# Layer 2's feed-forward up projections as seven quarter products instead of eight

## The chip, the cores and the metric

The kernel runs on one core of a Trainium2 chip. The core has five engines that work from queues of their own, each in order: TensorE (PE) for matmuls, VectorE (DVE), ScalarE (ACT), GpSimd (POOL) and SyncE (SP), which issues most DMA transfers here. The metric is the device time of one execution in microseconds (us); lower is better.

## The reference, cut to what matters

Two layers of a diffusion backbone over 512 latent tokens of width 1024, with 256 context tokens. Each layer has token mixers, an output projection with a gated residual, and a SwiGLU feed-forward part with 2816 inner columns. The change is in the second layer, where only the 512 latent tokens are still needed:

```python
def _swiglu(h, w1, w3, w2):
    return (jax.nn.silu(h @ w1) * (h @ w3)) @ w2
...
x = x + ga1 * (o @ w_out)
h2 = _rmsnorm(x, g_norm2) * (1.0 + sc2) + sh2
x = x + ga2 * _swiglu(h2, w_ff1, w_ff3, w_ff2)
```

All of it is in float32.

## The kernel before, in words

Activations lie transposed: 128 partitions hold 128 of the 1024 features, eight such tiles (k = 0 to 7) make the width, and tokens lie along the free dimension. A float32 product is made from three matmuls in a faster format (fp32r). Each operand is split into a high part (a cast) and a low part (the operand minus its high part), and `mm3` (the matmul is its line L241) issues high x high, high x low and low x high into one PSUM tile. Activations are split once; weights are split when they come in. `weights` does that: a transfer from SP's queue into a `raw` tile of 128 x 1024 (two buffers), a cast on ACT to `hi` (L231) and a subtraction on POOL to `lo` (L232), each with four buffers. It is shared by all weights of the program.

`dense` does the output projection and the feed-forward part of a layer. For layer 2 it first finishes the output projection in two halves of 256 tokens, with the sums of squares for the norm on the way; `norm_apply` then makes the scaled rows `xn` (DVE, L329) and the high (ACT, L331) and low part (DVE, L332) of h2 in two big tiles. The feed-forward loop goes over 22 blocks f of 128 inner columns, in groups of 3 or 4 (FF_CUTS). For each f, 8 k x 3 matmuls of 512 columns make the block of h2 @ w1 and as many that of h2 @ w3, each in a PSUM tile of its own. ACT applies Silu (L1331), DVE multiplies (L1332), ACT and DVE split the result into `gh` (L1335) and `gl` (L1337). After the group, `down` adds up its blocks' products with w2 for each of the eight output tiles, and `update` (DVE, L1248) multiplies by the gate and adds to x, in place. The last group's updates are followed by the transfers to the output.

What is issued when is decided by a scheduler at build time, which fixes an order for each engine; on the chip each engine runs its own queue in that order and waits on semaphores. A pool's buffer is given again when all that use its former tile are done. Only weights are marked as of high priority.

## Time and profile before

| what | value |
|---|---|
| median of 3 runs | 1828.52 us (1824.92 to 1829.95) |
| profiled execution, its own time | 1835.55 us |
| its span, first to last instruction | 1833.8 us |
| mean granted TensorE clock in it | 0.967 |
| PE, DVE, ACT, POOL busy in the span | 94%, 53%, 29%, 30% |

The profile comes from one execution, which took 7.0 us longer than the median of the runs; 1.75 us of its time lie outside the span. Busy times of an engine are sums over its instructions, and matmuls overlap each other, so the pace of matmuls is read from their starts and not from their durations. The granted clock is TensorE's, as a share of 2.4 GHz; it has two levels, 2.4 and 1.2 GHz.

### The profile page before, as it was taken

Reading aid. Unit: us, or ns where it says so; the run is one execution under the profiler, and the core shown is the slowest. Engines: PE = TensorE matmul, PEld = TensorE weight load, DVE = VectorE, ACT = ScalarE, POOL = GpSimd, SP = SyncE. Lnnn points to the kernel's source line nnn. Section 1 sums busy time; section 2 is a strip of 40 time slices with the busy share of each in tenths; the row PEclk is TensorE's granted clock in tenths of the full one; section 3 lists DMA queues with packets and bytes.
Section 4 is the critical chain, followed back from the end, with each engine's and each line's share of the span. In section 5 each row is a group of like instructions: output and inputs, shape, how many; then the busy total and the mean of one; then the engine's idle time right before and its main releaser. Section 6 shows DMA issues by size and latency. Waiting matters only on the chain.

```text
span 1833.8 us, 25688 instructions
## 1 busy us (share of the span) xinstructions
PE 1725.8 (94%) x10142; PEld 1395.3 (76%) x10142; DVE 969.5 (53%) x2259; ACT 527.2 (29%) x852; POOL 558.6 (30%) x360
## 2 busy tenths in 40 slices
PE   5899999898999999999899998989999999999999
PEld 2667877566878888888678877778767787787887
DVE  7988535572177445446956346265666632232332
ACT  2422234452241211121121223323444432222221
POOL 4553200201221322231643512423111244344442
PEclk7999989999999999999899998989999999999999
DMA  8355340414135434343342332332322123233222
GB/s 337 103 155 165 128 167 24 167 53 182 38 125 151 127 127 153 107 154 110 106 110 75 106 112 81 132 110 89 114 64 64 47 92 93 77 107 103 93 92 81
DMA packets 83065, 207.25 MB, mean 113 GB/s; under 512 B 15360, under 2 KB 35968, under 8 KB 82816
## 3 DMA queue, kind: packets, MB, share of 16 engines
q1 hardware_dynamic: 54160, 160.44, 26.9%
q0 software_dynamic: 7824, 29.38, 4.8%
q10 hardware_dynamic: 20960, 15.78, 2.8%
q8 instruction: 80, 1.31, 0.3%
q14 instruction: 41, 0.34, 0.1%
HBM read 185.68 MB, written 21.99 MB: 113 GB/s over the span
## 4 chain that ended last, share of the span: by engine, by line
PE 76%; DVE 15%; issue 4%; ACT 2%; POOL 1%; DMA 1%; ACTq 0%; DVEq 0%; POOLq 0%
PE psD L241 54%; PE psD L703 4%; PE psS L932 3%; PE psT L241 2%; PE psQ L979 1%; PE psQ L990 1%; PE psT L376 1%; PE psS L801 1%; POOL lo L232 1%; PE psT L856 1%; PE psQ L1045 1%; DVE ro L662 1%; PE psQ L1030 1%; PE psT L278 1%; PE psT L1067 1%
## 5 line engine op out<-in xcount | busy, mean ns | idle before, releaser
L232 POOL TENSOR_TENSOR lo<-raw,hi 128x1024 fp32r<-128x1024 f32 (+1 forms) x178 | 432.2, 2434 | 875.5 <-ACT hi L231 875.2
L241 PE MATMUL psD<-big,hi 128*128 128x512 f32 (+1 forms) x2368 | 605.9, 360 | 12.2 <-ACT big L331 5.7
L241 PEld LDWEIGHTS psD<-big,hi 128*128 128x128 f32 x2368 | 399.8, 191 | 88.1 <-ACT big L331 8.1
L231 ACT CAST hi<-raw 128x1024 fp32r<-128x1024 f32 (+1 forms) x178 | 184.2, 1039 | 774.5 <-PE psD L241 466.6
L241 PE MATMUL psD<-big,lo 128*128 128x512 f32 (+1 forms) x1184 | 368.2, 359 | 1.2 <-POOL lo L232 1.2
L241 PEld LDWEIGHTS psD<-big,lo 128*128 128x128 f32 x1184 | 202.9, 191 | 38.4 <-POOL lo L232 2.7
L1332 DVE TENSOR_TENSOR sg<-sg,psD 128x768 f32<-128x768 f32 (+1 forms) x44 | 36.1, 820 | 308.8 <-PE psD L241 300.5
L241 PE MATMUL psD<-gh,hi 128*128 128x512 f32 (+1 forms) x528 | 163.6, 359 | 4.9 <-DVE xb L1248 4.7
L241 PE MATMUL psD<-gl,hi 128*128 128x512 f32 (+1 forms) x528 | 165.8, 360 | 0.0
L241 PE MATMUL psD<-gh,lo 128*128 128x512 f32 (+1 forms) x528 | 163.6, 358 | 0.0
L1248 DVE SCALAR_TENSOR_TENSOR xb<-psD,mod,xb 128x512 f32<-128x512 f32 (+1 forms) x112 | 64.7, 613 | 114.9 <-PE psD L241 114.8
L1337 DVE TENSOR_TENSOR gl<-sg,gh 128x768 fp32r<-128x768 f32 (+1 forms) x44 | 99.2, 2254 | 39.5 <-ACT gh L1335 39.5
L407 DVE CUSTOM_DVE_ANT_0 junk<-wmt,cb,pcol 128x1024 f32<-128x1024 f32 x64 | 97.1, 1517 | 27.3 <-DMA wmt<-in_wmodT 26.2
L241 PEld LDWEIGHTS psD<-gh,hi 128*128 128x128 f32 x528 | 89.5, 189 | 24.4 <-DVE xb L1248 8.5
L241 PEld LDWEIGHTS psD<-gh,lo 128*128 128x128 f32 x528 | 90.1, 189 | 16.6 <-issue 0.2
L241 PEld LDWEIGHTS psD<-gl,hi 128*128 128x128 f32 x528 | 89.8, 189 | 15.8 <-issue 0.4
L1248 DVE SCALAR_TENSOR_TENSOR xq<-psD,mod,xq 128x512 f32<-128x512 f32 (+1 forms) x64 | 42.2, 682 | 78.6 <-PE psD L241 78.6
L932 PE MATMUL psS<-k,q 64*128 64x256 f32 (+1 forms) x432 | 78.2, 336 | 3.4 <-DVE mx L1019 3.0
L241 PE MATMUL psD<-h,hi 128*128 128x512 f32 (+1 forms) x288 | 76.2, 350 | 4.2 <-ACT h L331 2.7
L932 PEld LDWEIGHTS psS<-k,q 64*128 64x128 f32 x432 | 58.1, 195 | 23.6 <-issue 9.1
L241 PEld LDWEIGHTS psD<-h,hi 128*128 128x128 f32 x288 | 50.7, 194 | 15.4 <-ACT h L331 3.2
L241 PE MATMUL psD<-on,hi 128*128 128x256 f32 (+1 forms) x176 | 51.6, 331 | 1.3 <-ACT on L1081 1.3
(396 smaller groups left out, 2494.5 us busy)
## 6 DMA issues: line engine op xcount, KB each, us to landing
raw<-in_w_ff SPq DMA_DIRECT2D x132, 512.0 KB, 3.5
wmt<-in_wmodT SPq DMA_DIRECT2D x48, 512.0 KB, 3.6
wm<-in_wmod SPq DMA_DIRECT2D x28, 512.0 KB, 6.0
raw<-in_winT SPq DMA_DIRECT2D x18, 512.0 KB, 3.6
room<-in_wmod SPq DMA_DIRECT2D x12, 512.0 KB, 11.4
nab<-in_nab SPq DMA_DIRECT2D x8, 640.0 KB, 4.2
rot<-trot POOLq DMA_DIRECT2D x8, 576.0 KB, 6.0
cf<-in_four POOLq DMA_DIRECT2D x8, 520.0 KB, 4.9
```

The lines of the kernel that those rows point to most:

```text
L231: nc.scalar.copy(hi, raw)
L232: nc.gpsimd.tensor_sub(lo, raw, hi)
L241: nc.tensor.matmul(o, lhsT=lhs[i], rhs=rhs[j][..., s], start=start and n == 0, stop=stop and n == 2)
L278: self.nc.tensor.matmul(dst, lhsT=src, rhs=self.ident, start=True, stop=True)
L376: nc.tensor.matmul(ps[32 * j:32 * j + 32], lhsT=self.cvec[:, k], rhs=ws[k // 2][:, k % 2], start=half == 0, stop=half == 1)
L407: nc.vector.tensor_tensor_reduce(junk, w, cb[:, i], 1.0, self.pcol[1][:, PC_B + f:PC_B + f + 1], op0=ALU.mult, op1=ALU.add, accum_out=mod[ ...
L662: v.tensor_mul(er[:, :, :, o], er[:, :, :, s], bcr)
L703: nc.tensor.matmul(ps, lhsT=h[i][:, k, tk], rhs=w[j][:, k % per], start=k == 0 and q == 0, stop=k == KT - 1 and q == 2)
L932: self.nc.tensor.matmul(dst, lhsT=q2[i][h, qc], rhs=view(k2[j][h]), start=n == 0, stop=n == 2)
L1248: self.nc.vector.scalar_tensor_tensor(x[:, m, sl], ps[:, sl], gate[:, m, i:i + 1], x[:, m, sl], op0=ALU.mult, op1=ALU.add)
L1332: nc.vector.tensor_mul(sg, sg, pp[1])
L1337: marks.append(nc.vector.tensor_sub(gl, sg, gh))
```

## The change

Layer 2 gets a function of its own, `dense_last`, in place of `dense`. Two inner blocks, f and f + 11, are made together. Seen as 2 x 2 quarters, the weights of such a pair are a11, a12 (block f, features 0 to 511 and 512 to 1023) and a21, a22 (block f + 11); the activations are b11, b21, b12, b22 (features by halves, tokens by halves of 256). Seven products of quarter size replace eight, in Winograd's form of Strassen's scheme: four sums of weight quarters (s1 to s4, on DVE, in each round), four sums of activation quarters (t1 to t4, made once before the loop, in place in the tile of x), and seven additions behind the products. A quarter product is 4 k x 3 matmuls of 256 columns.

Weights of w1 and w3 are loaded by `load_halves` into `raw` and a second tile `raw2` (two buffers, in the loop's own pool), and split by `split_weight`, which makes the low part on DVE (L1371) where `weights` has it on POOL. w2 still goes through `weights`. The residual after the output projection is written to a tile of its own (`xr`) instead of over x. The down projection takes the two blocks of a pair at once and adds to `xr`; it uses the two PSUM tiles that were the norm's, and the up products have six instead of four.

```diff
@@ -1363,6 +1363,176 @@
+    def split_weight(self, src, n):
+        nc = self.nc
+        hi = self.whi.tile([P, n], F32R, name="hi")
+        lo = self.wlo.tile([P, n], F32R, name="lo")
+        nc.scalar.copy(hi, src)
+        nc.vector.tensor_sub(lo, src, hi)
+        return [(hi[:, i:i + 512], lo[:, i:i + 512]) for i in range(0, n, 512)]
+
+    def load_halves(self, fp, src, f):
+        nc = self.nc
+        with self.tc.high_priority():
+            ra = self.raw.tile([P, 1024], F32, name="raw")
+            rb = fp.tile([P, 1024], F32, name="raw2", bufs=2)
+            for t, g in ((ra, f), (rb, f + NFF // 2)):
+                nc.sync.dma_start(t, src[g].rearrange("p k c -> p (k c)"))
+        return ra, rb
+
+    def split_halves(self, fp, raws, part):
+        v = self.nc.vector
+        a1, a2 = (raws[0][:, i:i + 512] for i in (0, 512))
+        b1, b2 = (raws[1][:, i:i + 512] for i in (0, 512))
+        with self.tc.high_priority():
+            if part == 0:
+                return self.split_weight(raws[0], 1024)
+            if part == 3:
+                return self.split_weight(b2, 512)
+            s = fp.tile([P, 1024], F32, name="ssum", bufs=4)
+            if part == 1:
+                v.tensor_add(s[:, :512], b1, b2)
+                v.tensor_sub(s[:, 512:], s[:, :512], a1)
+                self.s2 = s[:, 512:]
+            else:
+                v.tensor_sub(s[:, :512], a1, b1)
+                v.tensor_sub(s[:, 512:], a2, self.s2_of)
+            return self.split_weight(s, 1024)
+
+    def dense_last(self, l, cl, on, x, hp, x_dst, parts):
...
+        res = hp.tile([P, KT, SEQ], F32, name="xr")
...
+                v.scalar_tensor_tensor(res[:, m, sl], ps[:, sl], mod[:, 16 + m, 0:1], x[:, m, sl],
+                                       op0=ALU.mult, op1=ALU.add)
...
+        def operand(name, src, gp):
+            hi, lo = (hp.tile([P, 4, HN], F32R, name=f"{name}{i}") for i in "hl")
+            nc.scalar.copy(hi, src)
+            (nc.gpsimd if gp else v).tensor_sub(lo, src, hi)
+            return hi, lo
+
+        B = {}
+        gsc = self.gsc[l][1]
+        for j, (pb, (sl, _)) in enumerate(zip(pbs, parts)):
+            for i in range(2):
+                for k in range(4 * i, 4 * i + 4):
+                    xn = self.xn.tile([P, NT], F32, name="xn")[:, :HN]
+                    v.scalar_tensor_tensor(xn, res[:, k, sl], gsc[:, k, 0:1], pb[:, :HN], op0=ALU.mult, op1=ALU.mult)
+                    nc.scalar.activation(x[:, k, sl], xn, AF.Identity, bias=sh[:, k, 0:1])
+                B[i, j] = x[:, 4 * i:4 * i + 4, sl]
+        ops = {1: operand("b11", B[0, 0], False), 2: operand("b21", B[1, 0], True)}
+        t1, t2, t3, t4 = B[0, 0], B[1, 1], B[0, 1], B[1, 0]
+        v.tensor_sub(t1, B[0, 1], B[0, 0])
+        ops[5] = operand("t1", t1, False)
+        v.tensor_sub(t3, B[1, 1], B[0, 1])
+        ops[3] = operand("b22", B[1, 1], True)
+        v.tensor_sub(t2, B[1, 1], t1)
+        ops[6] = operand("t2", t2, False)
+        ops[7] = operand("t3", t3, True)
+        v.tensor_sub(t4, B[1, 0], t2)
+        ops[4] = operand("t4", t4, True)
+        cl.close()
+
+        with tc.tile_pool(name=f"ff{l}", bufs=1) as fp:
+            tmp = lambda: fp.tile([P, HN], F32, name="pc", bufs=10)
+            for f in range(NFF // 2):
+                raws = [self.load_halves(fp, a[nm][l], f) for nm in ("w_ff1", "w_ff3")]
+                W, S2, u = [{}, {}], {}, [{}, {}]
+                sg = fp.tile([P, 2, SEQ], F32, name="sg", bufs=2)
+                c3 = fp.tile([P, 2, SEQ], F32, name="c3")
+                cs = (sg, c3)
+
+                def need(q, part, names):
+                    if part == 2:
+                        self.s2_of = S2[q]
+                    for nm, t in zip(names, self.split_halves(fp, raws[q], part)):
+                        W[q][nm] = [u.rearrange("p (k c) -> p k c", c=P) for u in t]
+                    if part == 1:
+                        S2[q] = self.s2
+
+                def prod(q, n, w):
+                    ps = self.psum((512,), "D")[:, :HN]
+                    for k in range(4):
+                        self.mm3([(ps, slice(0, HN))], [t[:, k] for t in W[q][w]], [t[:, k] for t in ops[n]],
+                                 k == 0, k == 3)
+                    return ps
+
+                def keep(q, name, ps=None, add=None):
+                    u[q][name] = tmp()
+                    if add is None:
+                        nc.scalar.copy(u[q][name], ps)
+                    else:
+                        v.tensor_add(u[q][name], u[q][add], ps)
+
+                for q in range(2):
+                    need(q, 0, ("a11", "a12"))
+                    keep(q, "p1", prod(q, 1, "a11"))
+                for q in range(2):
+                    need(q, 1, ("s1", "s2"))
+                    v.tensor_add(cs[q][:, 0, :HN], u[q]["p1"], prod(q, 2, "a12"))
+                for q in range(2):
+                    keep(q, "p5", prod(q, 5, "s1"))
+                for q in range(2):
+                    need(q, 2, ("s3", "s4"))
+                    keep(q, "u2", prod(q, 6, "s2"), "p1")
+                    keep(q, "u5", u[q]["p5"], "u2")
+                for q in range(2):
+                    v.tensor_add(cs[q][:, 0, HN:], u[q]["u5"], prod(q, 3, "s4"))
+                    if q == 0:
+                        nc.scalar.activation(sg[:, 0], sg[:, 0], AF.Silu)
+                for q in range(2):
+                    need(q, 3, ("a22",))
+                    ps = prod(q, 7, "s3")
+                    v.tensor_add(cs[q][:, 1, HN:], u[q]["u5"], ps)
+                    keep(q, "u3", ps, "u2")
+                v.tensor_mul(sg[:, 0], sg[:, 0], c3[:, 0])
+                gt = []
+
+                def halves(i):
+                    gh = fp.tile([P, SEQ], F32R, name="gh", bufs=4)
+                    gl = fp.tile([P, SEQ], F32R, name="gl", bufs=4)
+                    nc.scalar.copy(gh, sg[:, i])
+                    v.tensor_sub(gl, sg[:, i], gh)
+                    gt.append((gh, gl))
+
+                halves(0)
+                for q in range(2):
+                    v.tensor_add(cs[q][:, 1, :HN], u[q]["u3"], prod(q, 4, "a22"))
+                    if q == 0:
+                        nc.scalar.activation(sg[:, 1], sg[:, 1], AF.Silu)
+                v.tensor_mul(sg[:, 1], sg[:, 1], c3[:, 1])
+                halves(1)
+                w2 = [self.weights(a["w_ff2"][l, g], (D,)) for g in (f, f + NFF // 2)]
+                for m in range(KT):
+                    ps = self.psum((SEQ,), "Q")
+                    for i in range(2):
+                        self.mm3([(ps, slice(0, SEQ))], [t[:, m * P:(m + 1) * P] for t in w2[i]], gt[i], i == 0, i == 1)
+                    self.update(res, mod[:, 40:48], m, ps, [(slice(0, SEQ), 0)])
+                    if f == NFF // 2 - 1:
+                        nc.sync.dma_start(x_dst[:, m], res[:, m])
+
@@ -1423,11 +1593,10 @@
         st = ExitStack()
         self.psum_pools(st, "p1", D=(2, 1024), S=(3, 512), T=(1, 512))
         cl, on, x = self.mixers(1, True, h, h1s, st, None, xd)
-        with cl, tc.tile_pool(name="hp2", bufs=1, side="right") as hp, ExitStack() as st:
-            big = lambda shape, dt: [hp.tile(shape, dt, name=f"big{i}", tag=f"big{i}") for i in range(2)]
-            self.psum_pools(st, "d1", D=(4, 512), Q=(2, 512), T=(2, 512))
+        with tc.tile_pool(name="hp2", bufs=1, side="right") as hp, ExitStack() as st:
+            self.psum_pools(st, "d1", D=(6, 512), Q=(2, 512))
             halves = [(slice(0, 256), 0), (slice(256, 512), 0)]
-            self.dense(1, True, cl, on, x, big, self.out, None, halves, None)
+            self.dense_last(1, cl, on, x, hp, self.out, halves)


 def _build(nc, tc, a, out, dump=None):
```

Three places in the order of instructions follow; names in them are the program's tiles.

VectorE, in the middle of the loop. Before, between the last updates of one group and the next blocks:

```order
L1248 SCALAR_TENSOR_TENSOR xq_11293<-psD_15184,mod1_92,xq_11293 128x512
L1248 SCALAR_TENSOR_TENSOR xq_11293<-psD_15195,mod1_92,xq_11293 128x512
L1332 TENSOR_TENSOR sg_15268<-sg_15268,psD_15219 128x512
L1337 TENSOR_TENSOR gl_15272<-sg_15268,gh_15271 128x512
L1332 TENSOR_TENSOR sg_15337<-sg_15337,psD_15288 128x512
L1337 TENSOR_TENSOR gl_15341<-sg_15337,gh_15340 128x512
```

After, from the first multiplication of one round (its products 7 and 4 are still to be added) to the low part of the next round's a11 and a12, the last row here:

```order
L1510 TENSOR_TENSOR sg<-sg,c_14024 128x512
L1508 TENSOR_TENSOR c_14024<-pc,psD 128x256
L1487 TENSOR_TENSOR pc<-pc,psD 128x256
L1394 TENSOR_TENSOR ssum<-raw_14372 128x512
L1522 TENSOR_TENSOR sg<-pc,psD 128x256
L1517 TENSOR_TENSOR gl<-sg,gh 128x512
L1522 TENSOR_TENSOR c_14024<-pc,psD 128x256
L1525 TENSOR_TENSOR sg<-sg,c_14024 128x512
L1398 TENSOR_TENSOR ssum<-raw,raw_14368 128x512
L1395 TENSOR_TENSOR ssum<-ssum,raw 128x512
L1517 TENSOR_TENSOR gl<-sg,gh 128x512
L1371 TENSOR_TENSOR lo<-raw,hi 128x1024
```

The weights' low parts and sums, of which VectorE had none, now stand in its queue among the additions behind the products. Five rows stand just ahead of these: two additions of product 3 (L1502), one more sum (L1394), and product 7's first addition and the row behind it (L1508, L1487).

TensorE, between two rounds. Before, where up products (with h2, the `big` tiles) end and a group's down products begin:

```order
L241 MATMUL psD_15426<-big1_13228,hi_15419 128x512
L241 MATMUL psD_15426<-big0_13227,lo_15421 128x512
L241 MATMUL psD_15506<-gh_15271,hi_15482 128x512
L241 MATMUL psD_15506<-gl_15272,hi_15482 128x512
L241 MATMUL psD_15506<-gh_15271,lo_15484 128x512
L241 MATMUL psD_15506<-gh_15340,hi_15488 128x512
```

After, from the last matmul of product 4 (with t4) over down products (psQ) to the next round's product 1 (with b11):

```order
L241 MATMUL psD_14272<-t4h_13301,lo_14233 128x256
L241 MATMUL psQ_14303<-gh_14253,hi_14291 128x512
L241 MATMUL psQ_14311<-gh_14253,hi_14291 128x512
L241 MATMUL psQ_14303<-gl_14254,hi_14291 128x512
L241 MATMUL psQ_14303<-gh_14253,lo_14293 128x512
L241 MATMUL psQ_14311<-gl_14254,hi_14291 128x512
L241 MATMUL psQ_14311<-gh_14253,lo_14293 128x512
L241 MATMUL psQ_14303<-gh_14287,hi_14297 128x512
L241 MATMUL psQ_14311<-gh_14287,hi_14297 128x512
L241 MATMUL psD_14381<-b11h_13273,hi_14377 128x256
L241 MATMUL psD_14381<-b11l_13274,hi_14377 128x256
L241 MATMUL psQ_14303<-gl_14288,hi_14297 128x512
```

Before, a group's down products began with blocks that were made long ago and only ended with the newest. Now the first down products use the block that has just been multiplied, and the next round's product 1 follows; the rest of the down products stands between products 1, 2, 5 and 6 of the next round.

GpSimd, from the last mixers to the end, as a difference:

```order
 L841 DMA cf_12054<-in_four 128x1040
-L232 TENSOR_TENSOR lo<-raw,hi 128x1024 x70
-L1448 UNCONDITIONAL_BRANCH
-L1448 ISA
+L232 TENSOR_TENSOR lo<-raw,hi 128x1024 x4
+L1433 TENSOR_TENSOR b21l<-xq,b21h 128x1024
+L1433 TENSOR_TENSOR b22l<-xq,b22h 128x1024
+L1433 TENSOR_TENSOR t3l<-xq,t3h 128x1024
+L1433 TENSOR_TENSOR t4l<-xq,t4h 128x1024
+L232 TENSOR_TENSOR lo<-raw,hi 128x1024 x22
```

Of 70 low parts of weights 26 are left, 22 of them those of w2; four low parts of activation quarters are new. The other three (b11, t1, t2) are VectorE's.

## Rows read from the trace of the kernel before

**Rows 1.** The page: parts 1 and 4, busy time and the chain that ended last.
```profile
PE 1725.8 (94%) x10142; PEld 1395.3 (76%) x10142; DVE 969.5 (53%) x2259; ACT 527.2 (29%) x852; POOL 558.6 (30%) x360
...
PE 76%; DVE 15%; issue 4%; ACT 2%; POOL 1%; DMA 1%; ACTq 0%; DVEq 0%; POOLq 0%
```

**Rows 2.** Stretches: start:end, length, busy us (instructions) by engine, granted clock, DMA share, GB/s.
```profile
core 0: us, PE busy (x) PEld busy (x) DVE busy (x) ACT busy (x) POOL busy (x), PEclk, DMA share, GB/s
...
1500.00:1800.00 300.00, 298.84 (x1279) 239.22 (x1279) 85.07 (x76) 73.39 (x88) 128.45 (x54) 1.00 0.30 93
```

**Rows 3.** Groups by form, 1510 to 1800: form, count | busy, mean ns | idle before.
```profile
L232 POOL TENSOR_TENSOR lo<-raw,hi 128x1024 fp32r<-128x1024 f32 x52 | 125.0, 2409 | 168.1 <-ACT hi L231 167.8
...
L1337 DVE TENSOR_TENSOR gl<-sg,gh 128x512 fp32r<-128x512 f32 x17 | 41.7, 2450 | 15.2 <-ACT gh L1335 15.2
...
L1335 ACT CAST gh<-sg 128x512 fp32r<-128x512 f32 x17 | 10.5, 620 | 0.0
```

**Rows 4.** Order of time (start, duration, engine, line), TensorE: first, last of 32 matmuls.
```profile
1431.96 0.28 PE L241 MATMUL psD<-lowaq,hi 128*128 128x256 f32 x1
...
1435.62 0.28 PE L241 MATMUL psD<-on,lo 128*128 128x256 f32 x1
```

**Rows 5.** Order of time, 1560 to 1620: VectorE, then GpSimd.
```profile
1561.38 2.43 DVE L1337 TENSOR_TENSOR gl<-sg,gh 128x512 fp32r<-128x512 f32 x1 [0.69 <-ACT gh L1335]
...
1572.58 2.43 DVE L1337 TENSOR_TENSOR gl<-sg,gh 128x512 fp32r<-128x512 f32 x1 [0.69 <-ACT gh L1335]
1579.29 2.07 DVE L1248 SCALAR_TENSOR_TENSOR xq<-psD,mod,xq 128x512 f32<-128x512 f32 x3 [4.28 <-PE psD L241]
...
1593.53 0.75 DVE L1248 SCALAR_TENSOR_TENSOR xq<-psD,mod,xq 128x512 f32<-128x512 f32 x1 [2.05 <-PE psD L241]
...
1560.87 2.41 POOL L232 TENSOR_TENSOR lo<-raw,hi 128x1024 fp32r<-128x1024 f32 x1 [3.20 <-ACT hi L231]
...
1592.36 4.75 POOL L232 TENSOR_TENSOR lo<-raw,hi 128x1024 fp32r<-128x1024 f32 x2 [17.89 <-ACT hi L231]
1599.57 2.41 POOL L232 TENSOR_TENSOR lo<-raw,hi 128x1024 fp32r<-128x1024 f32 x1 [2.46 <-ACT hi L231]
```

**Rows 6.** Groups by form over the whole span: VectorE, ScalarE.
```profile
L602 DVE TENSOR_TENSOR ot<-ot,o 128x576 f32<-128x576 f32 x8 | 6.0, 745 | 1.1 <-POOL o L600 1.1
...
L600 DVE TENSOR_TENSOR ot<-sm,scd 128x1152 f32<-128x1152 f32 x4 | 5.4, 1346 | 0.0
...
L952 DVE TENSOR_TENSOR aq<-psQ,xn 128x256 f32<-128x256 f32 x10 | 4.2, 422 | 19.3 <-PE psQ L990 19.3
...
L920 DVE TENSOR_TENSOR aq<-aq,xn 128x512 f32<-128x512 f32 x4 | 2.7, 678 | 0.0
...
L949 ACT COPY xn<-psQ 128x256 f32<-128x256 f32 x20 | 7.4, 368 | 11.4 <-PE psQ L278 11.4
```

**Rows 7.** Order of time, ScalarE: a cast that waits for its weights.
```profile
1605.74 1.05 ACT L231 CAST hi<-raw 128x1024 fp32r<-128x1024 f32 x1 [2.24 <-DMA raw<-in_w_ff]
```

**Rows 8.** Start of the part: busy time by stretch; order of time, three engines.
```profile
1448.00:1452.00 4.00, 1.78 (x18) 1.04 (x16) 1.46 (x7) 2.62 (x4) 2.72 (x2) 1.00 0.00 0
1452.00:1456.00 4.00, 2.57 (x14) 2.49 (x15) 4.00 (x12) 1.87 (x4) 1.94 (x1) 0.71 0.66 171
1456.00:1460.00 4.00, 4.00 (x21) 4.00 (x21) 3.93 (x17) 1.95 (x5) 0.00 (x0) 0.50 0.23 93
1460.00:1464.00 4.00, 3.36 (x26) 3.16 (x26) 1.82 (x6) 0.91 (x2) 0.00 (x0) 0.94 0.00 0
...
1452.65 0.51 PE L241 MATMUL psD<-big,hi 128*128 128x256 f32 x2 [1.19 <-ACT big L331]
...
1454.54 0.47 DVE L329 SCALAR_TENSOR_TENSOR xn<-xq,gsc,psQ 128x256 f32<-128x256 f32 x1
...
1452.09 0.91 ACT L331 ACTIVATE big<-xn,mod 128x256 fp32r<-128x256 f32 x2 [1.32 <-DVE xn L329]
```

**Rows 9.** Order of time, TensorE: the last matmul.
```profile
1829.57 0.40 PE L241 MATMUL psD<-gh,lo 128*128 128x512 f32 x1
```

23 lines of the change are left out of this document (added).

## The prediction

> **What bounds the kernel now.** I read the page first [rows 1]: TensorE (PE) is busy for 94% of the span and holds 76% of the chain that ended last. Then the table by stretches over layer 2's feed-forward part [rows 2]: 298.84 of 300 us of PE are busy at granted clock 1.00, while VectorE (DVE) is busy for 85, ScalarE (ACT) for 73 and GpSimd (POOL) for 128. Nothing but PE limits this stage, so fewer PE cycles are worth their time there as long as nobody else becomes late. One up block takes 11.20 us (`gl` starts at 1561.38 and again at 1572.58 [rows 5]), that is 48 matmuls of 512 columns at 0.2333 us, and DVE works for little of it. The pace of 256 columns stands in [rows 4]: 31 steps from 1431.96 to 1435.62, 0.118 us each. Two halves cost 0.236 against 0.2333, so narrow products are nearly free on PE, weight loads included.
>
> **PE work.** A pair of blocks takes 96 matmuls up and 48 down before: 144 x 0.2333 = 33.6 us. After, 2 x 84 matmuls of 256 columns x 0.118 = 19.8, and 48 down = 11.2: 31.0 us. Eleven pairs: 28.6 us less. That is all that the change can win, and only where PE never waits.
>
> **DVE work of a pair, after.** Durations from [rows 6]: 0.42 for 256 columns with one operand in PSUM, 0.68 for 512 with two in SBUF. 1024 columns with two SBUF operands don't stand there; between 576 (0.745) and 1152 (1.346) the slope gives an estimate of 1.21. For each of w1 and w3: four weight sums of 512 (2.72), three `lo` of 1024 and one of 512 (4.31), seven combinations of 256 (2.94): 9.97, twice 19.9. Two multiplications and two `gl` of 512: 2.7. Eight updates at 0.75 [rows 5]: 6.0. Sum 28.7 us in a round whose PE work is 31.0. Before, 85.07 in 300 us [rows 2] make 9.5 in 33.6, `gl`'s waits (see next) included. DVE becomes as loaded as PE.
>
> **POOL shuts DVE out.** In [rows 5] the `gl` that starts at 1561.38 ends at 1563.81, 0.53 after POOL's `lo` ends (1560.87 + 2.41 = 1563.28): it lasts 2.43 where the 0.68 of [rows 6] would do. Its mean over 17 is 2.450 [rows 3]. The update of 1593.53, which has an operand in PSUM, lies in the midst of POOL's work (1592.36 to 1597.11) and takes 0.75. So operations with two SBUF operands wait for POOL, others don't. After, 22 of DVE's 42 operations of a round are of that kind, and POOL still has two `lo` of w_ff2 at 2.41 [rows 3, 5]: 0 to 4.8 us more for DVE, by where they fall.
>
> **The seam between two rounds.** Tiles' places decide it: `hi` and `lo` have four buffers, and s1/s2, s3/s4 and w_ff2 of one matrix follow each other in the same one. So the cast of w_ff2's first block waits for product 7, and POOL's two `lo` fall into products 4 and what follows, where DVE has its longest queue. I walk one round from the moment when `lo` of the first a11 is there (0). PE has 166 matmuls of 256 and 40 of 512 until product 4 ends: 19.6 + 9.3 = 28.9, without a wait that I can find (s1/s2 are split while the down products run between, s3/s4 likewise). Product 3 of w3 ends at 24.7. From there DVE's order (the first place in the section on the change) must get through seven combinations of 256 (2.9), four weight sums (2.7), two multiplications and two `gl` (2.7) and the `lo` of the next round's a11 (1.2) before PE can go on with product 1: 9.5, so 34.2 at the least. The casts of `gh` (0.62 [rows 3]) and the second Silu lie beside these. POOL's 4.8 put wholly on top give 39.0. With the times of the walk (casts of w_ff2 at 25.1 and 26.2, `lo` until 28.6 and 31.6, DVE's first multiplication and its second sum held by them) 3.1 of it land on the queue: 37.3. A second chain nearly joins it: w1's next tile goes into the buffer that POOL's first `lo` frees at 28.6, lands and is cast 3.76 later as from 1601.98 (1599.57 + 2.41 [rows 5]) to 1605.74 [rows 7], so the cast begins at 32.4, and the `lo` behind it is not late. Of the 8.4 us from 28.9 to 37.3 PE has work for 2.2 (8 down matmuls, 2 of product 1). The rows that PE has in hand there are the second place in the section on the change: nothing of the next round but two matmuls stands ahead of that `lo`.
>
> **The clock.** In [rows 8] PE is busy for 1.78 of 4 us from 1448 on; the granted clock is then 0.71, 0.50 and 0.94 in the next three stretches of 4 us. As it has two levels, 1.2 and 2.4 GHz, the lower held for 2.3, 4.0 and 0.5 us, in most of which PE was busy: some 6 us of work that would have taken 3. A seam with 2.2 of 8.4 us busy is emptier than the stretch from 1448. Price 0 to 3.0 a round; PE is busy again just after, but part of the slow time falls into DVE's queue, and the short seams may not trip it: I take 1.2. Period: 37.3 + 1.2 = 38.5 (bounds 34.2 and 42.0).
>
> The Trainium skill, page "TensorE: Matmul & The Clock Gate", section "HAM oscillation — how this bites in real kernels", has a loop that pays for the fall of the clock in every pass because PE waits once a pass. By that rule all ten seams would cost 3.0, a period of 40.3; the rows show one such fall, so I leave it as a rival.
>
> **First round and end.** Before, PE's first product of this part starts at 1452.65 and the last ends at 1829.8 (1829.57 and one pace) [rows 8, 9]: 377.1 for 11 x 33.6 = 369.6, so 7.5 lost at the start. After, product 1 waits for four scaled rows, their biases and one cast of 1024 instead of one (b11 high at 1455.4, low at 1456.6); 24 matmuls at the low clock bring 1461; the second half's eight rows (0.47 on DVE, 0.91 for two on ACT [rows 8], two buffers) 1466.5. Then the cast of the last operand (1.05 as in [rows 7]), and the operands follow one another through the shared place of xq: DVE's t1 low, t3, t2, t4, t2 low and POOL's b22, t3, t4 (the third place) are 5 x 1.21 + 3 x 2.41 = 13.3, of which hardly two can overlap since both engines want the same operands' port: 1480.5 with that cast. The copy of product 1 waits for POOL's t4 low (its tile lies where xq was), then two copies (0.37 [rows 6]), two combinations, seven weight sums and one `lo`: 7.5, so product 5 starts at 1488. Five products of both matrices, 120 x 0.118 = 14.2, and 2.4 for the clock: product 4 ends at 1504.6. The residual in a tile of its own costs nothing: its write is the same update that was there. The last round has no next weights in its seam, so 5.6 of the 9.5, which with POOL's 3.1 ends at 33.4, 4.5 after product 4; 42 down matmuls behind it are 9.8: 14.3.
>
> **Sum.** End of PE's work: 1504.6 + 10 x 38.5 + 14.3 = 1903.9, against 1829.8: 74.1 later. On the profiled execution, 1835.55, that makes 1909.6; the runs' median, 1828.52, lies 7.0 below it: 1902.6, I say 1902.
>
> **Rivals.**
> - *PE stays the bound, and the kernel is faster.* It needs DVE's seam queue to be ready when product 4 ends, so a period of 31.0. With the first round as above the end is 1504.6 + 310 + 14.3 = 1828.9, no change (1828); with a first round no worse than before (7.5 lost) 1452.65 + 7.5 + 341 = 1801.2, 28.6 less: 1800. For it: DVE's sum is below PE's. Against: the seam's chain hangs on products 3 and 4 of the same round. It decides where the period is below 31.1.
> - *POOL's `lo` and the clock cost nothing:* period 34.2 to 35, 1856 to 1865.
> - *The clock falls at every seam:* period 40.3, end 1921.9, so 1921; with POOL wholly on top 42.0, 1938.
> - *A little better than the forecast all along,* a seam half hidden, period 31.5 to 34: 1833 to 1855. Against: each price is from single operations, and back-to-back ones overlap by some 0.06 (three updates in 2.07 [rows 5]); that is 0.9 of the 9.5, not 3.
>
> **Chances.** The forecast (1866 to 1912) 0.45; clock at every seam 0.19; no lock and no clock 0.17; seam half hidden 0.07; above 1938 0.01; no change 0.04; faster 0.07. Range: from 1850, which takes the bound of the seam's queue with a little overlap, to 1938. A measurement of this kernel can tell 0.3%, 5.5 us, from no change: faster 0.07, same 0.04, slower 0.89.
>
> **What would show it.** Right: stretches of some 38 us repeating eleven times after 1500, each with 5 to 8 us in which PE is idle behind DVE `lo` L1371 or `gl` L1517, granted clock below 1.00 there; DVE above 70% busy in this stage; `lo` or sums on DVE of 2 to 3.5 us where POOL runs; PE's matmuls of this part fewer in time by 28.6. Wrong: PE's busy share near 1.00 in this stage, or a period near 31. If the waits are named for DMA (raw) rather than DVE, the second chain was the longer one. If the first product 5 starts near 1475, the first round was overpriced by 13.

## The result and the profile after

The changed kernel takes 1889.0 us (median of 4 runs, 1885.9 to 1896.8) against 1829.2 before: 1.0343 times as long, 95% interval 1.0319 to 1.0366. The profiled execution took 1896.78 us, 61.2 more than that of before.

The page of after, parts 1 and 4, beside [rows 1]:

```profile
PE 1726.7 (91%) x10886; PEld 1429.2 (75%) x10886; DVE 1194.3 (63%) x2620; ACT 588.7 (31%) x947; POOL 468.9 (25%) x320
...
PE 69%; DVE 19%; issue 5%; DMA 3%; ACT 2%; POOL 2%; ACTq 0%; DVEq 0%; POOLq 0%
```

The chain that ended last went from PE (76% to 69%) to VectorE (15% to 19%) and transfers (1% to 3%). Four of the ten stretches between the ends of product 4 (columns as in [rows 2]):

```profile
1545.30:1581.70 36.40, 33.37 (x218) 30.07 (x217) 28.95 (x43) 13.44 (x18) 3.74 (x3) 0.95 0.26 84
1581.70:1618.20 36.50, 33.40 (x218) 29.80 (x217) 29.51 (x46) 13.76 (x19) 5.11 (x3) 0.95 0.29 87
1618.20:1654.30 36.10, 32.30 (x219) 29.05 (x217) 29.15 (x40) 12.61 (x17) 6.43 (x3) 1.00 0.30 93
...
1801.80:1839.40 37.60, 34.47 (x218) 31.14 (x216) 29.48 (x43) 13.43 (x18) 3.89 (x3) 0.91 0.26 81
```

A round takes 36.7 us in the mean of ten (35.4 to 37.7). VectorE is busy for about 29 of them (80%) where [rows 2] had 28%, and the granted clock is below 1.00 in nine of ten. One seam in PE's order of time:

```profile
1581.61 0.27 PE L241 MATMUL psD<-t4h,lo 128*128 128x256 f32 x1
1582.55 0.73 PE L241 MATMUL psQ<-gh,hi 128*128 128x512 f32 x2 [0.67 <-ACT gh L1516]
1585.60 0.50 PE L241 MATMUL psQ<-gl,hi 128*128 128x512 f32 x1 [2.32 <-DVE gl L1517]
...
1586.21 0.63 PE L241 MATMUL psQ<-gl,hi 128*128 128x512 f32 x1
1586.64 0.63 PE L241 MATMUL psQ<-gh,lo 128*128 128x512 f32 x1
...
1588.40 0.51 PE L241 MATMUL psD<-b11h,hi 128*128 128x256 f32 x1
...
1590.13 0.28 PE L241 MATMUL psD<-b11h,lo 128*128 128x256 f32 x1
```

Product 4 ends at 1581.73. PE waits for `gh`, then 2.3 us for `gl`. From 1586.1 to 1589.5 it runs at the lower clock (matmuls of 512 columns 0.43 us apart), and product 1 flows from 1590.13 on: 8.4 us in which it did fourteen matmuls, twelve of 512 columns and two of 256. VectorE and GpSimd in the same seam:

```profile
1577.48 0.42 DVE L1502 TENSOR_TENSOR c<-pc,psD 128x256 f32<-128x256 f32 x1 [0.98 <-PE psD L241]
...
1579.54 2.30 DVE L1510 TENSOR_TENSOR sg<-sg,c 128x512 f32<-128x512 f32 x1
1581.77 0.41 DVE L1508 TENSOR_TENSOR c<-pc,psD 128x256 f32<-128x256 f32 x1
1582.10 0.41 DVE L1487 TENSOR_TENSOR pc<-pc,psD 128x256 f32<-128x256 f32 x1
1582.43 2.19 DVE L1394 TENSOR_TENSOR ssum<-raw 128x512 f32<-128x512 f32 x1
1584.54 0.41 DVE L1522 TENSOR_TENSOR sg<-pc,psD 128x256 f32<-128x256 f32 x1
1584.87 0.68 DVE L1517 TENSOR_TENSOR gl<-sg,gh 128x512 fp32r<-128x512 f32 x1
...
1587.80 0.68 DVE L1517 TENSOR_TENSOR gl<-sg,gh 128x512 fp32r<-128x512 f32 x1
1588.40 1.22 DVE L1371 TENSOR_TENSOR lo<-raw,hi 128x1024 fp32r<-128x1024 f32 x1
...
1578.90 5.17 POOL L232 TENSOR_TENSOR lo<-raw,hi 128x1024 fp32r<-128x1024 f32 x2 [32.66 <-PE psD L241]
```

VectorE has hardly a gap from 1578.27 to the low part of the next a11. While GpSimd works (1578.90 to 1584.07) its two operations with two SBUF operands take 2.30 and 2.19 us instead of 0.68, 3.1 us in all; those with an operand in PSUM take 0.41 as ever. The Trainium skill, page "SBUF — State Buffer", section "SBUF: two separate sides", has one port pair that GpSimd and such VectorE operations lock for a whole instruction; the trace agrees, 2.30 and 2.19 against 0.68.

The first round, in four engines' order of time:

```profile
1460.94 0.79 PE L241 MATMUL psD<-b11h,hi 128*128 128x256 f32 x2 [3.08 <-ACT b11h L1432]
...
1491.32 0.58 PE L241 MATMUL psD<-t1h,hi 128*128 128x256 f32 x1 [21.19 <-ACT hi L1370]
...
1494.32 0.58 PE L241 MATMUL psD<-t1h,hi 128*128 128x256 f32 x1 [2.21 <-ACT hi L1370]
...
1477.20 3.35 DVE L1451 TENSOR_TENSOR xq<-xq 128x1024 f32<-128x1024 f32 x1 [2.23 <-POOL b22l L1433]
...
1488.77 0.69 DVE L1394 TENSOR_TENSOR ssum<-raw 128x512 f32<-128x512 f32 x1 [2.28 <-DMA raw<-in_w_ff]
...
1482.97 2.34 POOL L1433 TENSOR_TENSOR t4l<-xq,t4h 128x1024 fp32r<-128x1024 f32 x1 [3.50 <-ACT t4h L1432]
...
1485.34 0.65 ACT L1485 COPY pc<-psD 128x256 f32<-128x256 f32 x2 [2.45 <-POOL t4l L1433]
```

Between products 2 and 5 PE waits for 21 us: t2 (L1451) waits for b22's low part and is then stretched by GpSimd's next one; the copies of product 1 wait for t4's low part; the weight sums wait for a raw tile that landed late.

**Dates of the two profiles.** One operation of GpSimd ahead of all that the diff touches, in before and in after:

```profile
1401.26 2.38 POOL L232 TENSOR_TENSOR lo<-raw,hi 128x1024 fp32r<-128x1024 f32 x1 [43.09 <-ACT hi L231]
```

```profile
1406.78 2.38 POOL L232 TENSOR_TENSOR lo<-raw,hi 128x1024 fp32r<-128x1024 f32 x1 [43.07 <-ACT hi L231]
```

It is 5.5 us later in after; in the experiments' profiles it lies anywhere from 1394 to 1408, so the change is not what moves it. I set these 5.5 us aside. Less 5.5:

| | predicted | after |
|---|---|---|
| product 1 starts | 1455.4 | 1455.4 |
| product 5 starts (w1, w3) | 1488 | 1485.8, 1488.8 |
| first product 4 ends | 1504.6 | 1504.4 |
| ten rounds | 385 | 366.9 |
| from the last product 4 to the last matmul | 14.3 | 13.9 |
| last matmul ends, against before's 1829.8 | 1903.9 (+74.1) | 1885.2 (+55.4) |

### The profile page after: what moved, and what is told of

Read it like the earlier page. It is cut to its first block, busy times and chain, and to the rows that moved or that the text cites. A ratio compares the mean times of both kernels' runs of the same rounds, so it can differ in the third digit from the quotient of the medians.

```text
span 1895.0 us, 27672 instructions
## 1 busy us (share of the span) xinstructions
PE 1726.7 (91%) x10886; PEld 1429.2 (75%) x10886; DVE 1194.3 (63%) x2620; ACT 588.7 (31%) x947; POOL 468.9 (25%) x320
## 4 chain that ended last, share of the span: by engine, by line
PE 69%; DVE 19%; issue 5%; DMA 3%; ACT 2%; POOL 2%; ACTq 0%; DVEq 0%; POOLq 0%
PE psD L241 42%; PE psQ L241 6%; PE psD L703 4%; PE psS L932 3%; PE psT L241 2%; PE psQ L979 1%; DMA wm<-in_wmod 1%; PE psQ L990 1%; PE psT L376 1%; PE psT L856 1%; PE psS L801 1%; PE psQ L1045 1%; DMA raw<-in_w_ff 1%; DVE sg L1510 1%; PE psT L265 1%
## 5 line engine op out<-in xcount | busy, mean ns | idle before, releaser
L232 POOL TENSOR_TENSOR lo<-raw,hi 128x1024 fp32r<-128x1024 f32 (+1 forms) x134 | 328.2, 2456 | 972.1 <-ACT hi L231 807.9
L241 PE MATMUL psD<-big,hi 128*128 128x512 f32 (+1 forms) x1632 | 380.0, 346 | 9.7 <-ACT big L331 3.9
L241 PEld LDWEIGHTS psD<-big,hi 128*128 128x128 f32 x1632 | 260.3, 190 | 54.9 <-DVE big L332 6.6
L241 PE MATMUL psD<-big,lo 128*128 128x512 f32 (+1 forms) x816 | 225.2, 343 | 0.0
L241 PEld LDWEIGHTS psD<-big,lo 128*128 128x128 f32 x816 | 132.4, 191 | 20.0 <-issue 1.0
L407 DVE CUSTOM_DVE_ANT_0 junk<-wmt,cb,pcol 128x1024 f32<-128x1024 f32 x64 | 97.7, 1527 | 28.3 <-DMA wmt<-in_wmodT 27.2
L241 PE MATMUL psD<-gl,hi 128*128 128x512 f32 (+1 forms) x352 | 97.2, 342 | 0.0
L241 PE MATMUL psD<-gh,lo 128*128 128x512 f32 (+1 forms) x352 | 95.9, 339 | 0.0
L241 PE MATMUL psQ<-gl,hi 128*128 128x512 f32 x176 | 74.8, 426 | 15.1 <-DVE gl L1517 15.1
L241 PE MATMUL psQ<-gh,hi 128*128 128x512 f32 x176 | 71.1, 427 | 15.6 <-ACT gh L1516 15.1
L241 PE MATMUL psQ<-gh,lo 128*128 128x512 f32 x176 | 73.4, 418 | 0.0
```

The costliest lines, as they stand in the source:

```text
L232: nc.gpsimd.tensor_sub(lo, raw, hi)
L241: nc.tensor.matmul(o, lhsT=lhs[i], rhs=rhs[j][..., s], start=start and n == 0, stop=stop and n == 2)
L407: nc.vector.tensor_tensor_reduce(junk, w, cb[:, i], 1.0, self.pcol[1][:, PC_B + f:PC_B + f + 1], op0=ALU.mult, op1=ALU.add, accum_out=mod[ ...
```

## The experiments

Ratios are to the kernel before; after itself is 1.0343 (1.0319 to 1.0366).

| | ratio, 95% interval | us |
|---|---|---|
| e1_no_lock | 1.0246 (1.0229 to 1.0263) | 1875.4 |
| e2_no_sums | 1.0159 (1.0134 to 1.0184) | 1857.6 |
| e3_lo_on_pool | 1.0573 (1.0527 to 1.0618) | 1936.0 |
| e4_down_later | 1.0102 (1.0071 to 1.0134) | 1847.2 |
| e5_no_lock_raw3 | 1.0285 (1.0236 to 1.0334) | 1877.5 |
| e6_rows_early | 1.0303 (1.0273 to 1.0332) | 1883.8 |
| e7_eight | 1.0129 (1.0095 to 1.0162) | 1851.7 |
| e8_later_early | 1.0056 (1.0034 to 1.0079) | 1839.0 |
| e9_all_dve | 1.0371 (1.0339 to 1.0403) | 1900.3 |
| e10_plain_first | 0.9999 (0.9982 to 1.0016) | 1828.1 |
| e11_first_dve | 0.9907 (0.9883 to 0.9931) | 1814.0 |
| e12_first_rows | 0.9928 (0.9903 to 0.9953) | 1814.6 |

### e1_no_lock: GpSimd out of the loop

```diff
-            nc.gpsimd.tensor_sub(lo, raw, hi)
+            if act:
+                nc.scalar.copy(lo, raw)
+            else:
+                nc.gpsimd.tensor_sub(lo, raw, hi)
...
+                w2 = [self.weights(a["w_ff2"][l, g], (D,), True) for g in (f, f + NFF // 2)]
```

> The low parts of the second feed-forward matrix are left out (a second cast on ScalarE fills their tiles), so GpSimd does nothing in the loop and ScalarE has 2.1 us more in a round. Theory A (a round lasts as long as PE's stretch from the low part of the next a11 to product 4, 29.3 us in the profile after, and VectorE's queue at the seam, 7.4, of which 3.1 to 3.7 are operations lengthened by GpSimd): the seam falls to about 4.0, the period from 36.7 to 33.3, the time from 1889 to 1850 to 1860. Rival C (the half clock behind each seam is what the rounds lose, up to 1.8 each): the clock still falls, under 10 us gained, 1880 or more. Rival D (the next tile of w1 comes late because its buffer is freed late by GpSimd): the buffer comes free 2 to 3 us earlier, and the time falls by more than VectorE's operations shrink.

13.6 us less instead of 29 to 39. Two rounds, then VectorE in the second of these seams:

```profile
1535.60:1569.60 34.00, 31.91 (x217) 29.20 (x216) 25.77 (x42) 15.11 (x20) 0.00 (x0) 1.00 0.24 70
1569.60:1607.60 38.00, 34.51 (x218) 31.42 (x218) 26.64 (x44) 15.07 (x22) 0.00 (x0) 0.91 0.31 105
```

```profile
1572.41 0.69 DVE L1397 TENSOR_TENSOR ssum<-raw 128x512 f32<-128x512 f32 x1 [2.32 <-DMA raw<-in_w_ff]
1573.02 0.68 DVE L1520 TENSOR_TENSOR gl<-sg,gh 128x512 fp32r<-128x512 f32 x1
```

The lock is real: without it six of the ten rounds take 33.7 to 33.9 us, about as worked out. But from the third round on every other one takes 37.8 to 38.1, at clock 0.91: a weight sum of the next round waits at the head of VectorE's queue for its transfer, and `gl`, whose operands are there, stands behind it. In the same seam ScalarE waits 3.4 us for a11's own tile. Theory A missed that one queue carries both.

### e2_no_sums: no weight sums

```diff
-            s = fp.tile([P, 1024], F32, name="ssum", bufs=4)
...
-            return self.split_weight(s, 1024)
+            return self.split_weight(raws[1 if part == 1 else 0], 1024)
```

> The eight weight sums of a round are left out: raw quarters are split in their place, so everything but VectorE's eight additions is done as before. Theory A: four of them stand in the seam's queue (2.4 us at their pace of 0.60), one of these lengthened by 1.5; the period falls by 2.4 to 3.3 and the first round by 2 to 4, 1889 to 1852 to 1864. Rival B (VectorE's whole sum of a round is the bound, wherever the operations stand): all eight count, 4.8 and the lengthening, the period falls by 5 to 6 to that of PE, 1830 to 1838. Rival C (clock): 1880 or more.

1857.6, in theory A's range; eight rounds of 33.9 to 34.0 us and two of 34.9, where theory B wanted 31. Two of them:

```profile
1639.80:1673.70 33.90, 32.02 (x218) 29.06 (x218) 24.15 (x35) 13.13 (x18) 5.19 (x3) 1.00 0.29 94
1673.70:1708.60 34.90, 33.06 (x218) 30.11 (x218) 24.16 (x35) 13.13 (x18) 5.19 (x3) 0.95 0.28 91
```

PE waits for the same 1.83 us in both; they differ by the clock alone, and by 1.0 us. That is what a fall of the clock costs a round when nothing hides it.

### e3_lo_on_pool: low parts of w1 and w3 on GpSimd

```diff
-        nc.vector.tensor_sub(lo, src, hi)
+        nc.gpsimd.tensor_sub(lo, src, hi)
```

> The low parts of w1's and w3's operands go to GpSimd as they did before the change. VectorE loses 8 us of work in a round, GpSimd gains 19 (8 at 2.41 or 1.2 each) and is busy for 24 of 36. Theory A: VectorE's 14 other operations with two SBUF operands are lengthened far more often, and the low part of the next a11 takes 2.4 instead of 1.2 behind those of w2: no gain, a period of 36 to 40, 1880 to 1925. Rival B (VectorE's sum is the bound): 8 us less there, the period falls to PE's 31 to 33, 1832 to 1852.

Slower still, 1936, above theory A's range; rounds of 42.0. Groups by form between 1500 and 1800, VectorE, then GpSimd (columns as in [rows 3]):

```profile
L1395 DVE TENSOR_TENSOR ssum<-ssum,raw 128x512 f32<-128x512 f32 x15 | 27.5, 1834 | 0.0
...
L1487 DVE TENSOR_TENSOR pc<-pc 128x256 f32<-128x256 f32 x14 | 15.2, 1083 | 1.5
```

```profile
L1371 POOL TENSOR_TENSOR lo<-raw,hi 128x1024 fp32r<-128x1024 f32 x16 | 43.3, 2721 | 27.5 <-ACT hi L1370 27.4
```

VectorE gave away eight low parts a round, and the rounds are 5.3 us longer than in after: a weight sum of 0.68 takes 1.83, an addition of 0.42 takes 1.08. Theory B falls.

### e4_down_later: down products one round later

```diff
+            def down(f, gt):
...
                 for q in range(2):
                     keep(q, "p5", prod(q, 5, "s1"))
+                if f:
+                    down(*last)
...
-                w2 = [self.weights(a["w_ff2"][l, g], (D,)) for g in (f, f + NFF // 2)]
...
+                last = f, gt
+            down(*last)
```

`down` holds the loop over m that stood at the round's end.

> All of the change is kept; only the down products of a pair are issued one round later, behind products 5 of the next pair, so that PE has work at the seam that waits for nothing new. Theory A: the seam's queue is hidden by 11.2 us of down products, the period falls from 36.7 to 31 to 32.5, and the time from 1889 to 1832 to 1848. Rival B (VectorE's sum with GpSimd's lengthening, 29 to 32 us busy of which little can be hidden, is the bound): the period stays above 34, 1862 or more. Rival C (clock): the clock stays at 1.00 when PE does not wait, and at most 1.8 a round of the gain is from it.

42 us less, in theory A's range; rounds of 32.4. The ten of them in one stretch:

```profile
1512.00:1836.00 324.00, 314.95 (x2152) 291.18 (x2152) 280.86 (x417) 129.37 (x179) 62.58 (x21) 1.00 0.32 95
```

VectorE still has all its work (280.86 of 324) and GpSimd's lock, yet PE is busy for 97% at clock 1.00. So VectorE's sum was not the bound (theory B); what PE waited for was that the first down products needed `gl` of the same round. With most of the waits the falls of the clock went too.

### e5_no_lock_raw3: e1 and a third `raw2`

```diff
-            rb = fp.tile([P, 1024], F32, name="raw2", bufs=2)
+            rb = fp.tile([P, 1024], F32, name="raw2", bufs=3)
```

> As e1_no_lock (the low parts of the second feed-forward matrix left out), and a third buffer for the second raw tile, whose transfer then need not wait for the split of a22 of the round before. In e1 periods of 33.9 and 37.9 us alternate; in the long ones the weight sum of w3 stands in VectorE's queue 2.3 us for its transfer, with gl behind it. Theory A2 (the seam's chain is VectorE's queue in order, and a transfer that is late holds it as well as GpSimd does): the long rounds go, all take about 33.9, 1875 to 1852 to 1860. Rival (the long rounds come from the other raw tile or from the clock, which is 0.91 in them): 1868 or more.

Not distinguishable from e1. The alternation went, as theory A2 said, but the rounds take 33.6 to 36.8, mean 35.4, not 33.9: the rival was right, though its two causes, the other tile and the clock (0.95 in five of the ten rounds), are not told apart. ScalarE in one seam:

```profile
1572.78 1.05 ACT L1373 CAST hi<-raw 128x1024 fp32r<-128x1024 f32 x1 [1.54 <-DMA raw<-in_w_ff]
1574.75 1.05 ACT L1373 CAST hi<-raw 128x1024 fp32r<-128x1024 f32 x1 [0.92 <-DMA raw<-in_w_ff]
```

Here a11's own tile is late: `raw` has two buffers, and w_ff2's blocks sit in them until they are split.

### e6_rows_early: operands out of the mixers' memory

```diff
+        cl.close()
         with tc.tile_pool(name=f"ff{l}", bufs=1) as fp:
+            B = {(i, j): fp.tile([P, 4, HN], F32, name="ssum", bufs=5) for i, j in ((0, 0), (0, 1), (1, 1), (1, 0))}
...
-                    nc.scalar.activation(x[:, k, sl], xn, AF.Identity, bias=sh[:, k, 0:1])
+                    nc.scalar.activation(B[i, j][:, k % 4], xn, AF.Identity, bias=sh[:, k, 0:1])
```

> All of the change is kept; the scaled rows and t1 to t4 lie in the tiles of the weight sums (five instead of four), so the mixers' memory is given back before the first round and not behind its last operand. Theory A (of the 21 us in which PE waits in the first round, the part behind the operands is due to copies, transfers and sums that wait for that memory): product 5 starts 5 to 12 us earlier, the rounds stay at 36.7, 1889 to 1877 to 1884. Rival (the chain of operands itself, through t1, t2 and t4 on two engines that share a port, sets product 5 and 6): within 4 us of 1889.

1883.8, in theory A's range by its time (its interval just touches that of after, so the dates say more), but only in part by its way. PE's first round, and VectorE and GpSimd where it waits:

```profile
1461.93 0.58 PE L241 MATMUL psD<-t1h,hi 128*128 128x256 f32 x1 [5.06 <-ACT hi L1370]
...
1473.82 0.58 PE L241 MATMUL psD<-t1h,hi 128*128 128x256 f32 x1 [8.13 <-ACT hi L1370]
...
1466.54 3.35 DVE L1452 TENSOR_TENSOR ssum<-ssum 128x1024 f32<-128x1024 f32 x1 [2.26 <-POOL b22l L1433]
...
1473.46 3.39 DVE L1433 TENSOR_TENSOR t2l<-ssum,t2h 128x1024 fp32r<-128x1024 f32 x1
```

Counted from the start of product 1, w1's product 5 starts after 14.2 us instead of 30.4, but w3's only after 26.0, and product 4 ends 5.9 us earlier: the rest of the 21 us is the chain through t2, with GpSimd's low parts in it, as the rival had it. The rounds behind it take 37.2 in this profile, so that some of the 5.9 is lost again.

### e7_eight: all but the scheme

```diff
+                def block(q, i, j):
+                    ps = self.psum((512,), "D")[:, :HN]
+                    for k in range(8):
+                        self.mm3([(ps, slice(0, HN))], [t[:, k % 4] for t in W[q][i][k // 4]],
+                                 [t[:, k % 4] for t in ops[k // 4, j]], k == 0, k == 7)
+                    return ps
...
+                for q in range(2):
+                    for j in range(2):
+                        nc.scalar.copy(cs[q][:, i, j * HN:(j + 1) * HN], block(q, i, j))
```

> The other parts of the change alone: pairs of blocks, products of 256 columns, a residual tile of its own, loads and low parts as after, but eight quarter products that add up in PSUM, so no sums of weights or activations and no additions behind the products (copies on ScalarE in their place). PE has 192 matmuls of 256 and 48 of 512 in a round, 33.9 us by the paces of the profile before; VectorE has 13.6. Theory A (what the change loses is VectorE's added work at the seam and in the first round, not the narrow products): PE bounds the loop at 34 to 35, the first round loses 6 to 12 more than before, 1838 to 1855. Rival E (256-column products with their weight loads are slower than their pace when all four operands alternate, or pairs and loads cost by themselves): a period above 36, over 1865.

1851.7, in theory A's range: rounds of 34.47 us, and PE is what bounds them:

```profile
1500.00:1800.00 300.00, 298.77 (x2097) 279.88 (x2096) 133.47 (x138) 97.74 (x158) 51.69 (x18) 1.00 0.32 92
```

Narrow products, pairs and the tile for the residual are nearly free in the loop (34.47 against 33.6). From the first product (1447.95) to the last matmul (1843.85) it is 395.9 us, against 377.1 in before: the eleven pairs are 9.6 (11 x 0.87) over PE's plain work, and 16.7 are lost (395.9 less 11 x 34.47) where before lost 7.5, nearly all of it in the first 20 us, where PE waits for the operands and the granted clock is 0.67.

### e8_later_early: e4 and e6

Its diff is that of e4 and that of e6 together.

> e4_down_later and e6_rows_early together. Theory A: the two losses (seam and first round) lie in different places and add up: 1847 less 5 to 12, 1835 to 1842, so still not below the kernel before. Rival: with the seam hidden VectorE is the bound at 28 of 32 us, and what is won in the first round is lost behind it: 1844 or more.

1839.0: the two gains add up (42 and 5 apart, 50 together by the medians), though its interval just touches that of e4. The rounds still take 32.5.

### e9_all_dve: low parts of w_ff2 on VectorE

```diff
-            nc.gpsimd.tensor_sub(lo, raw, hi)
+            (nc.vector if dve else nc.gpsimd).tensor_sub(lo, raw, hi)
...
+                w2 = [self.weights(a["w_ff2"][l, g], (D,), True) for g in (f, f + NFF // 2)]
```

> The change as it is, but the low parts of the second feed-forward matrix are made on VectorE too (in the loop GpSimd does nothing, nothing is left out). VectorE has two more operations of 1024 in a round, 2 x 1.14 at the pace of back-to-back ones, and loses the 3.1 to 3.7 us by which GpSimd's 5 us lengthened its own. Theory A (GpSimd's help costs VectorE more than it saves, but what e1 showed holds as well: behind the lock the next raw tile's transfer is nearly as late): a little better, 1872 to 1886. Rival (an engine that takes 5 us of work off VectorE's hands is worth it): 2.3 us more in the seam's queue in each of ten rounds, 1905 to 1915.

Both theories missed: 1900.3, not distinguishable from after. VectorE's operations are short again, and from the end of product 4 to the low part of the next a11 it is 5.7 us in the mean instead of 7.4; but the rest of the round takes 31.4 instead of 29.3, 37.1 in all. ScalarE in every second seam:

```profile
1551.02 1.04 ACT L1370 CAST hi<-raw 128x1024 fp32r<-128x1024 f32 x1 [5.21 <-DMA raw<-in_w_ff]
1551.97 0.62 ACT L1524 ACTIVATE sg<-sg 128x512 f32<-128x512 f32 x1
1553.03 1.04 ACT L1370 CAST hi<-raw 128x1024 fp32r<-128x1024 f32 x1 [0.43 <-DMA raw<-in_w_ff]
```

It stands 4.0 to 5.2 us at the head of its queue for the raw tile of a11, with the second Silu, and so `gl`, behind it; the next raw tile is late too, and the clock is 0.91 in most rounds. In the one round at clock 1.00 the rest takes 29.5, against 28.3 in the one such round of after, so the clock is not all of it. How the 2.1 us divide among these, and why the tiles land later than in after, stays open.

### e10_plain_first: the first pair by eight products

This is built on e8, with down products a round later and operands out of the mixers' memory.

```diff
+            for j, (pb, (sl, _)) in enumerate(zip(pbs, parts)):
...
+                for i in range(2):
+                    at = slice(j * HN, j * HN + HN)
+                    nc.scalar.activation(sg[:, i, at], block(0, i, j), AF.Silu)
+                    v.tensor_mul(sg[:, i, at], sg[:, i, at], block(1, i, j))
...
-            for f in range(NFF // 2):
+            for f in range(1, NFF // 2):
```

> e8_later_early, with the first of the eleven pairs made by eight products that add up in PSUM, which need only the splits of b11, b21, b12, b22; t1 to t4 and their splits are made beside those products. PE has 2.6 us more of work in that pair. Theory A (of what e8 still loses, some 13 us are waits of PE in the first round for the chain t1, t2, t4): 1839 less 6 to 12, 1827 to 1833, level with the kernel before. Rival (VectorE, not the chain, is what PE waits for at the start): within 4 us of 1839.

1828.1, level with before, in theory A's range.

### e11_first_dve: e10 with w_ff2's low parts on VectorE

The diff is that of e9, on e10.

> e10_plain_first, with the low parts of the second feed-forward matrix on VectorE as in e9. In e8's loop PE waits for about 1 us a round, for low parts of VectorE and GpSimd (2.4 to 3.5 us each there). Theory A (the lock costs VectorE as much as the two operations): within 5 us of e10, and the waits named for GpSimd's low part are gone. Rival (VectorE is full with 28 of 32 us, and 2.3 more make it the bound): 10 us or more above e10.

14 us less than e10, better than either theory, and below the kernel before by 0.7 to 1.2%. The stretch from 1500 to 1800 in e10, then in e11:

```profile
1500.00:1800.00 300.00, 290.85 (x1984) 268.52 (x1983) 261.00 (x387) 118.86 (x164) 52.56 (x18) 1.00 0.32 95
```

```profile
1500.00:1800.00 300.00, 298.27 (x2037) 276.58 (x2037) 266.07 (x416) 122.15 (x168) 0.00 (x0) 1.00 0.33 96
```

And one group of VectorE's in it, e10 first:

```profile
L1371 DVE TENSOR_TENSOR lo<-ssum,hi 128x1024 fp32r<-128x1024 f32 x37 | 59.2, 1610 | 7.3 <-ACT hi L1370 7.3
```

```profile
L1371 DVE TENSOR_TENSOR lo<-ssum,hi 128x1024 fp32r<-128x1024 f32 x36 | 43.6, 1217 | 2.7 <-ACT hi L1370 2.7
```

Rounds of 31.2 us, PE busy for 99.4%. The same move that was worth nothing in e9 is worth 14 us here, where PE has the down products of the round before to do at the seam.

### e12_first_rows: e11 with two low parts behind b11's

```diff
-                    with tc.high_priority():
+                    with tc.high_priority(), tc.issue_after(lows[0].ins) if i else ExitStack():
```

> e11_first_dve, with the casts and low parts of the first pair's second raw tiles placed behind b11's low part in the queues of ScalarE and VectorE. In e11 they stand ahead of half of b11's rows, and their tiles land late: VectorE waits 1 us and works 2.4 us for them, and PE's first product starts at 1451.7 with 6 us of waiting. Theory A (an operation that waits at the head of VectorE's queue holds the rows behind it): the first product starts 3 us earlier against the end of the output projection, 1814 to 1808 to 1812. Rival (the wait only moves behind the first 12 matmuls, where PE then needs those weights): 1812 to 1816.

1814.6, not distinguishable from e11. The edit moved VectorE's part alone; on ScalarE the cast stayed ahead of the rows and waits there:

```profile
1448.47 1.04 ACT L1370 CAST hi<-raw 128x1024 fp32r<-128x1024 f32 x1 [1.50 <-DMA raw<-in_w_ff]
```

VectorE, without the low parts ahead of its rows, then waits 1.8 us for ScalarE's. So theory A was not tried by this run. What moving both would give stays open.

## Why the prediction was right, and where it was off

**Direction and mechanism: right.** PE's work fell as said (a round of e11 is 31.2 us where e7's eight products take 34.47, 3.3 less; said: 33.6 to 31.0), and the seam ate it. e4 shows that it is the seam: with the same products, the same sums and the same lock, and only the down products elsewhere, 42 of the 60 us are gone.

**First round: right, 1504.4 against 1504.6,** and so was its way (copies behind t4's low part, the chain through t2). That the two agree to 0.2 us is luck: product 5 of w1 starts 2.2 us earlier and that of w3 0.8 us later than the 1488 of the walk, and the transfer that the sums wait for, 2.3 us, was not in it. e6 shows that the memory holds 5.9 us of this round; the rest of the wait is the chain.

**POOL shuts DVE out: right,** 2.5 to 3.7 us a round, 3.2 in the mean, against 3.1, and in e1 six of the ten rounds fall to 33.9 without it. What the walk left out is what e1, e5 and e9 found: several chains end at the seam close to one another. The "second chain" (w1's raw tile) was named and found not to be late by itself; in e5 and e9 it is, once the first is shortened, and in e1 w3's second raw tile is late as well. So taking the lock away alone did not give the rival without lock and clock, 34.2 to 35: e1's rounds average 35.5, and the clock still falls in four of them.

**The period: 38.5 against 36.7,** the step that was off, and by its sizes. Its first term, PE's work from the low part of a11 to the end of product 4, was walked as 28.9. In the one round whose clock kept 1.00 it takes 28.3, from the end of the first of these lines (1626.02) to the end of the second (1654.33, its start and one pace):

```profile
1624.80 1.22 DVE L1371 TENSOR_TENSOR lo<-raw,hi 128x1024 fp32r<-128x1024 f32 x1
...
1654.21 0.28 PE L241 MATMUL psD<-t4h,lo 128*128 128x256 f32 x1
```

Twelve down matmuls of 512 columns stand before that low part there, where the walk had eight. e2's eight rounds at clock 1.00 have 28.3 to 28.4 as well. The clock was priced at 1.2. It fell in nine rounds of ten, and the mean of ten for this part is 29.3, so the falls cost at most about 1.0 a round; some of that is down matmuls, since 36 to 41 of them are left behind the low part in those nine rounds and 36 in this one. 32 of the 41 us at half clock lie ahead of the low part, where PE waits for VectorE anyway. e2 prices a fall at 1.0 where nothing hides it. The seam was priced at 8.4 and measures 7.4: operations back to back start 0.33, 0.60 and 1.14 us apart, not 0.42, 0.68 and 1.22, which is 1.35 us in the queue's 16 operations (0.9 was named, for a rival). The three differences (0.6, 0.2 and 1.0) make 18 us in ten rounds. In the two profiles the 5.5 us ahead of the part go the other way.

**The rivals.** PE stays the bound: e11's rounds show that it can, but not with the down products at the round's end. The clock at every seam, 3.0 a round: it falls in nine of ten, at about a third of that price. The Trainium skill, page "TensorE: Matmul & The Clock Gate", section "HAM oscillation — how this bites in real kernels", has a loop that pays for the fall in every pass. The trace nearly agrees on how often, nine rounds of ten.

**The signs.** VectorE busy for 80%, waits named for `gl` L1517, stretches of 1.6 to 2.9 us under GpSimd's low parts: as listed. PE's idle time in a seam is 2.0 to 3.8 us, not the 5 to 8 listed: in the rest of the seam it does 7 to 12 down matmuls, many of them at half clock. Waits of PE for `gh` (ScalarE) were not listed; the product that `gh` casts is itself one of the stretched operations (L1510).

## What to carry to other kernels

When a change trades matmuls for vector work, look at what stands between the last product of one round and the first of the next: if a consumer of the round's own result comes first there, all of the new work is exposed, however much room the engines have on average. Shortening one chain at such a place shows the next; giving PE work that depends on the round before (e4) hides most of them, and only then did moving the low parts of w_ff2 to VectorE pay. An operation that waits for a transfer holds everything behind it in its engine's queue (2.3 us in e1, 4.0 to 5.2 in e9). Work given to GpSimd is not all taken off VectorE: in after two low parts of 2.4 us there lengthen VectorE's operations by 3.2 us a round, more than the 2 x 1.14 that it needs for them itself. The Trainium skill, page "Perfetto Trace Analysis", section "Optimizing Scalar/DVE Operations", says that moving work between these two might not help. The runs agree and go further: moving w1's and w3's low parts to GpSimd costs 47 us in e3, and moving w_ff2's the other way gains 14 in e11, though nothing in e9.

## What the runs showed that I had not expected

- The lock goes both ways: two low parts of GpSimd in a row take 5.17 us in a busy seam where they took 4.75 before [rows 5].
- The clock fell after waits shorter than I had thought of: in e2, with a single wait of 1.83 us a round, in two rounds of ten; in after, with 2.0 to 3.6 us in one to three pieces, in nine, while the one other round, with 3.8, kept 1.00.
- Moving the same two operations from GpSimd to VectorE was worth nothing in e9 and 14 us in e11.
